# Sixty-four slots for four experts in place of three, wide and narrow experts in turn, and a narrow block's transposes inside the next block's products

## The chip, the cores and the metric

The kernel runs on one core of a Trainium2 chip. The time is that of one execution on the device, in microseconds (us). A profile is one execution taken by the hardware profiler; its times are counted from the first instruction of the span. PE is the matrix engine (TensorE), PEld its weight load, DVE the vector engine, ACT the scalar engine, POOL GpSimd, and SP the engine that issues the loads.

## The reference

A two-layer network on 256 latent and 256 context tokens of 1024 numbers in fp32. Layer 0 (scans and a dense feed-forward part) and the attention of layer 1 are not touched by the change. What it touches is the last stage: each of the 256 latent tokens goes to two of eight experts, and every expert has its own weights.

```python
def swiglu(h, w_gate, w_up, w_down):
    return (jax.nn.silu(h @ w_gate) * (h @ w_up)) @ w_down

def moe(h, w_router, w_gate, w_up, w_down):
    logits = (h @ w_router).astype(jnp.float32)
    top_val, top_idx = lax.top_k(logits, TOP_K)          # TOP_K = 2
    top_w = jax.nn.softmax(top_val, axis=-1)
    combine = jnp.sum(jax.nn.one_hot(top_idx, N_EXPERTS, dtype=jnp.float32) * top_w[..., None], axis=-2)
    out = jnp.zeros_like(h)
    for e in range(N_EXPERTS):                           # 8 experts, 1024 x 3584 gate, up; 3584 x 1024 down
        out = out + combine[..., e:e + 1].astype(h.dtype) * swiglu(h, w_gate[e], w_up[e], w_down[e])
    return out
```

With the reference's own inputs (seed 0) its routing sends 60, 52, 39, 90, 48, 47, 107 and 69 tokens to experts 0 to 7.

## The kernel before, in words

**Slots.** An expert's tokens are gathered into slots. `sorted` ranks the experts by their number of tokens (expert 0 always first, the others by falling count), so that number n in the program is a place in that ranking and `ids` holds which expert it is. `SLOTS` gives each place 128 slots (`CAP`) or 64 (`HALF`), and `ORDER` says in which order the places are worked through. In this kernel places 0 to 4 have 128 slots and places 5 to 7 have 64. Where an expert has more tokens than slots, `more` is above zero and a second pass under `tc.If(more > 0)` at the end of `experts` does the rest.

**Wide and narrow.** `expert` (128 slots, called wide here) splits each 128x1024 fp32 piece of weights into two fp32r parts (`wsplit`, ACT L183 and DVE L184) and multiplies three times (`mm3`, L194 to L196). `expert_half` (64 slots, called narrow) multiplies the fp32 weights as they are (L1427 gate and up, L1445 down), the two halves of the output's partitions side by side; the trace shows each such product as two records. Both work in the same steps: seven blocks of gate and up, each of eight 128x1024 pieces; the gather of the next expert (`gather`, L1351 to L1367); 28 pieces of down; and then the spreading of the result over the tokens (L1510 and L1511, or L1458) and its sum (`moe`).

**A narrow block.** After a block's products, ACT takes the silu (L1430), DVE multiplies (L1432), PE transposes twice (L1435) and ACT stores the transposed block in `ef` (L1436), from which down reads it.

**Weights.** `raw2` loads two pieces (1024 KB, written 1 MB below) at a time, on SP's queue (L1388, and L176 as two loads of 512 KB). The places are used in a ring of ten such units: two in the `raw` buffers and eight in four `wide` tiles of two units each. A load waits on SP until the unit that was there is used up. An expert has 42 units (28 gate and up, 14 down); 42 x 1024 KB are 44.04 MB. SP issues strictly in order, and the order of the units does not depend on which experts are narrow.

The order of instructions on each engine is set by a scheduler that takes the program's order as priority, so pieces of one step can stand inside another.

Of the kernel before, what the change touches and what calls it, by code (L numbers as in the profile page):

```python
# [13 lines left out]
I32 = mybir.dt.int32  # L14
AF = mybir.ActivationFunctionType
# [4 lines left out]
P = 128  # L20
# [5 lines left out]
NE = 8  # L26
CAP = P
HALF = 64

ORDER = (0, 1, 7, 2, 6, 3, 4, 5)  # L30
SLOTS = (CAP,) * 5 + (HALF,) * 3
FE = 3584
LAM_INIT = 0.8 - 0.6 * math.exp(-0.3)

# [1128 lines left out]
class Layer1Experts(Layer1):  # L1163
# [72 lines left out]
    def experts(self):  # L1236
        nc = self.nc
        v = nc.vector
        self.nraw, self.wide, self.al_slot, self.rest_slot = -5, (2, 3, 0, 1), 4, 4
        self.place, self.eid = self.rank, [0] * NE  # L1240
        g = self.gather(0, 0)
        self.sorted()
        for i, n in enumerate(ORDER):
            if n:
                self.eid[n] = nc.values_load(self.ids[0:1, n:n + 1], engines=[mybir.EngineType.SP],
                                             min_val=0, max_val=NE - 1)
            nxt = ORDER[i + 1] if i + 1 < NE else None
            run = self.expert if SLOTS[n] == CAP else self.expert_half
            g = run(n, g, 0, nxt, not i, nxt is None)

        more = nc.values_load(self.more[0:1, 0:1], min_val=0, max_val=256)
        with self.tc.If(more > 0):
            self.nraw, self.wide, self.al_slot = 0, (3, 0, 1), 2
            for n in range(NE):
                self.expert(n, self.gather(n, SLOTS[n]), SLOTS[n], None, not n, False)
            for t in range(2):
                for j in range(2):
                    c = slice(512 * j, 512 * j + 512)
                    u = self.scr("s3")
                    v.tensor_tensor(u, self.moe[:, t, c], self.rest[:, 2, c], op=ALU.mult)  # L1260
                    self.put(t, c, u)

    def sorted(self):

        nc = self.nc
        v = nc.vector
        room = self.pc.tile([P, 384], F32, name="order", tag="dt_ex")
        at = [0]

        def new(shape):  # L1270
            n = math.prod(shape)
            at[0] += n
            r = room[:, at[0] - n:at[0]]
            return r.rearrange("p (a b) -> p a b", b=shape[1]) if len(shape) == 2 else r

        e8 = lambda ap: ap[:, None, :].to_broadcast([P, NE, NE])
        io = self.con[:, C_IO:C_IO + NE]
        pn = self.tr()
        for t in range(2):
            nc.tensor.matmul(pn[:, 0:NE], self.con[:, C_ONE:C_ONE + P], self.sel[:, t, :], start=t == 0, stop=t == 1)  # L1280
        cnt, key, pos = (new([NE]) for _ in range(3))
        v.tensor_copy(cnt, pn[:, 0:NE])
        v.tensor_copy(key, pn[:, 0:NE])
        v.tensor_scalar(key[:, 0:1], key[:, 0:1], 1024.0, None, op0=ALU.add)
        cmp = self.scr("s3", (P, 2, NE, NE))
        mine, other = key[:, :, None].to_broadcast([P, NE, NE]), e8(key)
        v.tensor_tensor(cmp[:, 0], other, mine, op=ALU.is_equal)
        v.tensor_tensor(cmp[:, 1], other, mine, op=ALU.is_gt)
        v.tensor_tensor(cmp[:, 0], cmp[:, 0], self.con[:, C_TIE:C_TIE + NE * NE].rearrange("p (a b) -> p a b", b=NE),
                        op=ALU.mult)  # L1290
        v.tensor_reduce(pos, cmp.rearrange("p i a b -> p a i b"), axis=AX.XY, op=ALU.add)
        v.tensor_scalar(pos, pos, 1.0, None, op0=ALU.add)

        hot = new([NE, NE])
        v.tensor_tensor(hot, e8(pos), io[:, :, None].to_broadcast([P, NE, NE]), op=ALU.is_equal)
        self.place, self.wts = (new([2, NE]) for _ in range(2))
        num = new([2, NE])
        u = self.scr("s3", (P, 2, NE, NE))
        for src, dst in ((self.rank, self.place), (self.cw, self.wts)):
            v.tensor_tensor(u, src[:, :, None, :].to_broadcast([P, 2, NE, NE]),  # L1300
                            hot[:, None].to_broadcast([P, 2, NE, NE]), op=ALU.mult)
            v.tensor_reduce(dst, u, axis=AX.X, op=ALU.add)
        v.tensor_tensor(u[:, 0], e8(io), hot, op=ALU.mult)
        v.tensor_tensor(u[:, 1], e8(cnt), hot, op=ALU.mult)
        v.tensor_reduce(num, u, axis=AX.X, op=ALU.add)
        v.tensor_scalar(num[:, 0], num[:, 0], -1.0, None, op0=ALU.add)
        self.ids = new([NE]).bitcast(I32)
        v.tensor_copy(self.ids, num[:, 0])
        for lo, hi, cap in ((0, 5, CAP), (5, NE, HALF)):
            v.tensor_scalar(num[:, 1, lo:hi], num[:, 1, lo:hi], -float(cap), None, op0=ALU.add)  # L1310
        top = new([1])
        v.tensor_reduce(top, num[:, 1], axis=AX.X, op=ALU.max)
        v.tensor_scalar(top, top, 0.0, None, op0=ALU.max)
        self.more = new([1]).bitcast(I32)
        v.tensor_copy(self.more, top)
# [89 lines left out]
    def expert_half(self, n, gathered, base, nxt, first, final):  # L1405

        nc = self.nc
        v = nc.vector
        mm = nc.tensor.matmul
        xg, pT, w_tok = gathered  # L1410
        sides = [slice(HALF * i, HALF * i + HALF) for i in range(2)]
        if final:
            self.rest = self.big(self.rest_slot, (P, 3, D), name="rest")
            self.row("odd", 5, 0, self.rest[:, 2])
        ap = self.big(5, (P, FE // P, HALF), name="ef")
        for b in range(FE // 512):
            if final and 2 <= b < 6:
                self.so_far(b - 2)
            ps = self.mm(b % 4)
            for u in range(0, KD, 2):  # L1420
                raw = self.raw2(self.weights("exp_gu", n, b, u // 2))
                for i in range(2):
                    k = u + i
                    for g in range(2):
                        for h, s in enumerate(sides):
                            c = 512 * g + 256 * h
                            mm(ps[s, 256 * g:256 * g + 256], xg[:, k, :], raw[i][:, c:c + 256],  # L1427
                               start=k + g == 0, stop=k == KD - 1, skip_group_check=True)
            sg = self.scr("s0", (P, 256))
            nc.scalar.activation(sg, ps[:, 0:256], AF.Silu)  # L1430
            t = self.scr("s3", (P, 256))
            v.tensor_tensor(t, sg, ps[:, 256:512], op=ALU.mult)  # L1432
            pt = self.tr()
            for f in range(2):
                nc.tensor.transpose(pt[:, P * f:P * f + P], t[:, P * f:P * f + P], self.ident)  # L1435
            nc.scalar.activation(ap[:, 4 * b:4 * b + 4, :].rearrange("p (h f) s -> p f h s", h=2),  # L1436
                                 pt[:, 0:256].rearrange("p (f h s) -> p f h s", f=2, h=2), AF.Copy)
        out = self.gather(nxt, base) if nxt is not None else None
        py = self.acc()
        nd = FE // P  # L1440
        for u in range(0, nd, 2):
            raw = self.raw2(self.weights("exp_d", n, u // 2))
            for f in (u, u + 1):
                for j, s in enumerate(sides):
                    mm(py[s], ap[:, f, :], raw[f - u][:, 512 * j:512 * j + 512], start=f == 0, stop=f == nd - 1,  # L1445
                       skip_group_check=True)
        y = self.scr("s2")
        if final:
            for j, s in enumerate(sides):
                v.scalar_tensor_tensor(y[s], py[s], w_tok[s], self.rest[s, 2, 512 * j:512 * j + 512],  # L1450
                                       op0=ALU.mult, op1=ALU.mult)
        else:
            nc.scalar.activation(y, py, AF.Copy, scale=w_tok)
        for t in range(2):
            for j, s in enumerate(sides):
                c = slice(512 * j, 512 * j + 512)
                pt = self.tr()
                mm(pt, pT[s, P * t:P * t + P], y[s], start=True, stop=True)  # L1458
                if final:
                    self.put(t, c, pt)  # L1460
                else:
                    v.tensor_tensor(self.moe[:, t, c], self.moe[:, t, c], pt, op=ALU.add)
        return out
# [73 lines left out]
```

## Time and profile before

| | |
|---|---|
| time, median of 3 runs | 2052.66 us (2048.9 to 2054.36) |
| the profiled execution's own time | 2045.38 us |
| its span | 2043.6 us |
| PE busy | 1973.8 us, 97% of the span |
| DVE, ACT busy | 1332.9 us, 997.5 us |
| moved by DMA | 502.69 MB, mean 246 GB/s |
| granted TensorE clock, mean | 0.991 of full speed |

The eight experts are the last 45% of the span. The profiled execution lies 1.8 us above its span and 7.3 us below the median of the runs. A busy share is an average over stages with different limits; the stages of the experts are read apart, by windows of time that begin with an expert's first product.

### The profile page before, as it was taken

What the parts mean: (1) busy time and instruction counts of PE and PEld (TensorE: products, weight loads), DVE (VectorE), ACT (ScalarE), POOL (GpSimd) and SP (SyncE); (2) the same over time, 40 slices, a digit from 0 to 9 for tenths busy, and PEclk for the clock granted to TensorE, in tenths of its full rate; (3) what the DMA queues carried; (4) which work ended last, traced back from release to release, by engine and by line L of the source; (5) the groups of instructions that cost most, each with busy time, mean ns of one, the idle gap of its engine ahead of it and who ended that gap; (6) DMA issues with size and microseconds to landing.
All of it is one profiled execution on the core that took longest, in us unless ns stands there. A gap on an engine that the chain in (4) does not pass through costs nothing.

```text
span 2043.6 us, 26783 instructions
## 1 busy us (share of the span) xinstructions
PE 1973.8 (97%) x9852; PEld 1496.0 (73%) x9852; DVE 1332.9 (65%) x2199; ACT 997.5 (49%) x1460; POOL 10.1 (0%) x12
## 2 busy tenths in 40 slices
PE   7999999999999999999999999998999999999997
PEld 4777778786888888877758787875488547888752
DVE  5468579755865565678566989960498109899700
ACT  5544346633332222255454887751487117888610
POOL 0000000000000000000000000000000000000010
PEclk9999999999999999999988999999999999999999
DMA  8333433433544555434405789989999999999897
GB/s 324 109 98 103 135 134 126 165 117 133 177 159 163 183 175 175 137 103 125 164 15 203 272 339 351 372 326 418 417 417 370 368 417 418 364 368 366 329 383 322
DMA packets 103867, 502.69 MB, mean 246 GB/s; under 512 B 13104, under 2 KB 13744, under 8 KB 69296
## 3 DMA queue, kind: packets, MB, share of 16 engines
q1 hardware_dynamic: 103728, 500.91, 65.5%
q8 instruction: 79, 1.29, 0.3%
q14 instruction: 60, 0.49, 0.1%
HBM read 495.62 MB, written 5.24 MB: 245 GB/s over the span
## 4 chain that ended last, share of the span: by engine, by line
PE 84%; DVE 7%; DMA 5%; ACT 3%; issue 1%; SPq 0%; ACTq 0%; DVEq 0%
PE mm L195 18%; PE mm L196 18%; PE mm L194 18%; PE mm L1427 7%; DMA wide<-exp_d 4%; PE acc L195 3%; PE acc L196 3%; PE acc L194 3%; DVE lo L184 2%; PE acc L315 1%; PE tr L1351 1%; PE acc L1445 1%; PE mm L1138 1%; PE tr L817 1%; PE acc L954 1%
## 5 line engine op out<-in xcount | busy, mean ns | idle before, releaser
L183 ACT ACTIVATE hi<-raw 128x1024 fp32r<-128x1024 f32 x240 | 254.0, 1060 | 411.1 <-PE mm L196 203.1
L184 DVE TENSOR_TENSOR lo<-wide,hi 128x1024 fp32r<-128x1024 f32 x336 | 407.5, 1223 | 42.3 <-ACT hi L183 15.7
L184 DVE TENSOR_TENSOR lo<-raw,hi 128x1024 fp32r<-128x1024 f32 x240 | 292.0, 1221 | 178.3 <-ACT hi L183 171.0
L183 ACT ACTIVATE hi<-wide 128x1024 fp32r<-128x1024 f32 x336 | 354.9, 1061 | 91.5 <-PE mm L196 59.5
L195 PE MATMUL mm<-lo,q 128*128 128x512 f32 x560 | 221.7, 396 | 2.3 <-DVE lo L184 2.3
L196 PE MATMUL mm<-hi,q 128*128 128x512 f32 x560 | 219.8, 393 | 0.0
L194 PE MATMUL mm<-hi,q 128*128 128x512 f32 x560 | 199.0, 392 | 0.0
L194 PE MATMUL mm<-hi,hh 128*128 128x512 f32 x416 | 168.8, 407 | 1.7 <-DVE b L856 1.3
L195 PE MATMUL mm<-lo,hh 128*128 128x512 f32 x416 | 164.9, 396 | 0.0
L196 PE MATMUL mm<-hi,hl 128*128 128x512 f32 x416 | 163.8, 396 | 0.0
L194 PE MATMUL mm<-h2h,hi 128*128 128x512 f32 (+1 forms) x376 | 142.2, 378 | 1.3 <-ACT hi L183 1.3
L195 PE MATMUL mm<-h2l,hi 128*128 128x512 f32 (+1 forms) x376 | 141.5, 377 | 0.0
L196 PE MATMUL mm<-h2h,lo 128*128 128x512 f32 (+1 forms) x376 | 141.1, 376 | 0.0
L1427 PE MATMUL mm<-wide,q 128*64 128x256 f32 x1072 | 127.6, 382 | 0.0
L195 PEld LDWEIGHTS mm<-lo,q 128*128 128x128 f32 x560 | 105.6, 189 | 29.7 <-DVE lo L184 7.0
L194 PEld LDWEIGHTS mm<-hi,q 128*128 128x128 f32 x560 | 105.3, 188 | 24.6 <-issue 1.6
L196 PEld LDWEIGHTS mm<-hi,q 128*128 128x128 f32 x560 | 105.7, 189 | 21.4 <-issue 0.8
L195 PE MATMUL acc<-lo,eh 128*128 128x512 f32 x280 | 110.2, 394 | 0.8 <-DVE lo L184 0.7
L1432 DVE TENSOR_TENSOR s<-s,mm 128x256 f32<-128x256 f32 x21 | 8.8, 421 | 154.7 <-ACT s L1430 154.7
L196 PE MATMUL acc<-hi,el 128*128 128x512 f32 x280 | 109.6, 391 | 0.0
L1427 PEld LDWEIGHTS mm<-wide,q 128*64 128x64 f32 x1072 | 77.1, 137 | 41.9 <-issue 6.0
L194 PE MATMUL acc<-hi,eh 128*128 128x512 f32 x280 | 101.9, 389 | 0.0
(392 smaller groups left out, 3301.5 us busy)
## 6 DMA issues: line engine op xcount, KB each, us to landing
wide<-exp_gu SPq DMA_DIRECT2D x177, 1024.0 KB, 8.9
wide<-exp_d SPq DMA_DIRECT2D x91, 1024.0 KB, 9.4
raw<-exp_gu SPq DMA_DIRECT2D x92, 512.0 KB, 10.0
raw<-odd_wmod SPq DMA_DIRECT2D x48, 512.0 KB, 4.4
raw<-w_in SPq DMA_DIRECT2D x44, 512.0 KB, 3.7
raw<-ffn_gu SPq DMA_DIRECT2D x44, 512.0 KB, 4.4
raw<-exp_d SPq DMA_DIRECT2D x42, 512.0 KB, 13.9
raw<-even_wmod SPq DMA_DIRECT2D x36, 512.0 KB, 3.7
```

The lines of the kernel that those rows point to most:

```text
L183: nc.scalar.activation(hi, raw, AF.Copy)
L184: nc.vector.tensor_tensor(lo, raw, hi.bitcast(F32), op=ALU.subtract)
L194: mm(ps, lh, rh, start=first, stop=False, skip_group_check=skip)
L195: mm(ps, lh, rl, start=False, stop=False, skip_group_check=skip)
L196: mm(ps, ll, rh, start=False, stop=last, skip_group_check=skip)
L315: nc.tensor.matmul(ps[r:r + 32, :], self.cond[:, k, :], raw[:, 512 * kk:512 * kk + 512], start=k < 4, stop=k >= 4)
L817: nc.tensor.matmul(pe, m, r.rearrange("p h l -> p (h l)"), start=d + i == 0, stop=d + i == 2)
L954: nc.tensor.matmul(py[:, w], l, r, start=i == 0, stop=i == len(prod) - 1)
L1138: nc.tensor.matmul(ps, self.qT1[r, h, qs], self.kT1[r, h, :], start=True, stop=True)
L1351: nc.tensor.matmul(pt[:, w * kk:w * kk + w], self.x[:, 2 + t, P * (k + kk):P * (k + kk) + P], pn[:, t, 0:w], start=t == 0, stop=t == 1)
L1427: mm(ps[s, 256 * g:256 * g + 256], xg[:, k, :], raw[i][:, c:c + 256], start=k + g == 0, stop=k == KD - 1, skip_group_check=True)
L1445: mm(py[s], ap[:, f, :], raw[f - u][:, 512 * j:512 * j + 512], start=f == 0, stop=f == nd - 1, skip_group_check=True)
```

## The change

Place 4 gets 64 slots instead of 128; the order of the places becomes 0, 7, 1, 6, 2, 5, 3, 4, so that a narrow expert follows each wide one. In a narrow expert, transposes and the store of block b are called between the second and the third pair of pieces of block b + 1, and those of the last block after the next expert's gather. The second pass takes only the experts that have tokens left (`extra`), and is cleared first.

```diff
-ORDER = (0, 1, 7, 2, 6, 3, 4, 5)
-SLOTS = (CAP,) * 5 + (HALF,) * 3
+ORDER = (0, 7, 1, 6, 2, 5, 3, 4)
+SLOTS = (CAP,) * 4 + (HALF,) * 4
...
         with self.tc.If(more > 0):
             self.nraw, self.wide, self.al_slot = 0, (3, 0, 1), 2
+            for t in range(2):
+                v.memset(self.moe[:, t, :], 0.0)
             for n in range(NE):
-                self.expert(n, self.gather(n, SLOTS[n]), SLOTS[n], None, not n, False)
+                extra = nc.values_load(self.extra[0:1, n:n + 1], min_val=-P, max_val=256)
+                with self.tc.If(extra > 0):
+                    self.expert(n, self.gather(n, SLOTS[n]), SLOTS[n], None, False, False)
...
-        for lo, hi, cap in ((0, 5, CAP), (5, NE, HALF)):
+        for lo, hi, cap in ((0, 4, CAP), (4, NE, HALF)):
             v.tensor_scalar(num[:, 1, lo:hi], num[:, 1, lo:hi], -float(cap), None, op0=ALU.add)
+        self.extra = new([NE]).bitcast(I32)
+        v.tensor_copy(self.extra, num[:, 1])
...
         ap = self.big(5, (P, FE // P, HALF), name="ef")
+        def turn(b, t):
+            pt = self.tr()
+            for f in range(2):
+                nc.tensor.transpose(pt[:, P * f:P * f + P], t[:, P * f:P * f + P], self.ident)
+            nc.scalar.activation(ap[:, 4 * b:4 * b + 4, :].rearrange("p (h f) s -> p f h s", h=2),
+                                 pt[:, 0:256].rearrange("p (f h s) -> p f h s", f=2, h=2), AF.Copy)
+
+        t = None
         for b in range(FE // 512):
...
                 raw = self.raw2(self.weights("exp_gu", n, b, u // 2))
+                if t is not None and u == 4:
+                    turn(b - 1, t)
...
             v.tensor_tensor(t, sg, ps[:, 256:512], op=ALU.mult)
-            pt = self.tr()
-            for f in range(2):
-                nc.tensor.transpose(pt[:, P * f:P * f + P], t[:, P * f:P * f + P], self.ident)
-            nc.scalar.activation(ap[:, 4 * b:4 * b + 4, :].rearrange("p (h f) s -> p f h s", h=2),
-                                 pt[:, 0:256].rearrange("p (f h s) -> p f h s", f=2, h=2), AF.Copy)
         out = self.gather(nxt, base) if nxt is not None else None
+        turn(FE // 512 - 1, t)
         py = self.acc()
```

**Where the instructions stand.** PE in the middle of the first narrow expert, before: a block is 32 products (`mm_...`), and behind its last one stand the two transposes of the same block's activations (`s_...`, L1435).

```order
L1435 MATMUL tr<-con,s_11475 128x128 x2
L1427 MATMUL mm_11481<-wide,q_10905 64x256 x32
L1435 MATMUL tr<-con,s_11522 128x128 x2
L1427 MATMUL mm_11528<-wide,q_10905 64x256 x8
L1427 MATMUL mm_11528<-raw,q_10905 64x256 x16
L1427 MATMUL mm_11528<-wide,q_10905 64x256 x8
L1435 MATMUL tr<-con,s_11574 128x128 x2
```

The same place with the change (products L1443, transposes L1425):

```order
L1443 MATMUL mm_10229<-wide,q_9806 64x256 x8
L1425 MATMUL tr<-con,s_10227 128x128 x2
L1443 MATMUL mm_10229<-wide,q_9806 64x256 x16
L1443 MATMUL mm_10279<-wide,q_9806 64x256 x16
L1425 MATMUL tr<-con,s_10277 128x128 x2
L1443 MATMUL mm_10279<-wide,q_9806 64x256 x16
L1443 MATMUL mm_10326<-wide,q_9806 64x256 x8
L1443 MATMUL mm_10326<-raw,q_9806 64x256 x8
L1425 MATMUL tr<-con,s_10324 128x128 x2
```

A block's transposes now stand 16 products into the next block; in later blocks the scheduler puts some of them 4 products in, or at the block's start.

PE at the end of gate and up of that expert, before: transposes, the next expert's gather (L1351 to L1367), then down (`acc`).

```order
L1427 MATMUL mm_11580<-wide,q_10905 64x256 x32
L1435 MATMUL tr<-con,s_11621 128x128 x2
L1351 MATMUL tr<-s_11630,x 128x128 x16
L1365 MATMUL tr<-con,m_11627 128x128 x2
L1367 MATMUL tr<-order,m_11627 128x1 x2
L1445 MATMUL acc<-wide,ef 64x512 x12
```

With the change (gather L1357 to L1373, down L1457):

```order
L1443 MATMUL mm_10474<-raw,q_9806 64x256 x4
L1425 MATMUL tr<-con,s_10472 128x128 x2
L1357 MATMUL tr<-s_10527,x 128x128 x2
L1443 MATMUL mm_10474<-raw,q_9806 64x256 x4
L1357 MATMUL tr<-s_10527,x 128x128 x10
L1443 MATMUL mm_10474<-wide,q_9806 64x256 x8
L1357 MATMUL tr<-s_10527,x 128x128 x4
L1371 MATMUL tr<-con,m_10524 128x128 x2
L1373 MATMUL tr<-order,m_10524 128x1 x2
L1443 MATMUL mm_10474<-wide,q_9806 64x256 x16
L1425 MATMUL tr<-con,s_10522 128x128 x2
L1457 MATMUL acc<-wide,ef 64x512 x20
```

The gather has moved into the last block, and the last block's transposes stand right behind its products with nothing between them and down.

## Rows read from the trace of the kernel before

**Rows 1.** The page: chain that ended last by engine; DMA and GB/s by slice.

```profile
PE 84%; DVE 7%; DMA 5%; ACT 3%; issue 1%; SPq 0%; ACTq 0%; DVEq 0%
...
DMA  8333433433544555434405789989999999999897
GB/s 324 109 98 103 135 134 126 165 117 133 177 159 163 183 175 175 137 103 125 164 15 203 272 339 351 372 326 418 417 417 370 368 417 418 364 368 366 329 383 322
```

**Rows 2.** Windows by expert: us, busy by engine, clock, DMA share, GB/s.

```profile
1239.90:1365.50 125.60, 125.26 (x580) 101.82 (x578) 112.15 (x107) 97.80 (x110) 0.00 (x0) 1.00 0.93 349
1365.50:1459.40 93.90, 86.73 (x622) 46.36 (x621) 8.36 (x18) 13.30 (x33) 0.00 (x0) 1.00 0.99 404
1459.40:1586.90 127.50, 126.65 (x577) 101.97 (x576) 112.24 (x105) 96.60 (x107) 0.00 (x0) 1.00 0.98 396
1586.90:1683.70 96.80, 88.63 (x623) 47.29 (x622) 8.95 (x18) 13.77 (x34) 0.00 (x0) 1.00 0.98 395
1683.70:1812.10 128.40, 127.68 (x577) 103.43 (x577) 114.59 (x108) 99.78 (x110) 0.00 (x0) 0.99 0.97 390
1812.10:1937.80 125.70, 124.98 (x579) 102.45 (x577) 111.33 (x104) 97.47 (x111) 0.00 (x0) 1.00 0.92 350
1937.80:2032.70 94.90, 84.70 (x591) 42.84 (x590) 7.21 (x15) 7.91 (x19) 9.90 (x8) 1.00 0.94 379
2032.70:2043.60 10.90, 3.95 (x8) 1.18 (x8) 4.22 (x6) 0.00 (x0) 0.00 (x0) 0.85 0.29 102
```

**Rows 3.** SP's own waits, of the wide expert from 1239.9 to 1365.5 us.

```profile
SPq L1388 <- DVE lo L184: 94.0, 18, 9.6
```

**Rows 4.** PE's waits (us in total, times, longest): first narrow expert, then the last.

```profile
PE tr L1435 <- DVE s L1432: 5.2, 6, 0.9
PE acc L1445 <- DMA wide<-exp_d: 1.1, 2, 0.6
...
PE acc L1445 <- DMA wide<-exp_d: 4.0, 7, 0.7
```

**Rows 5.** Windows inside experts, columns as in rows 2.

```profile
1365.00:1380.00 15.00, 14.94 (x108) 7.97 (x108) 4.56 (x8) 2.41 (x6) 0.00 (x0) 1.00 0.88 334
1380.00:1459.00 79.00, 71.89 (x520) 38.53 (x516) 4.30 (x10) 10.49 (x26) 0.00 (x0) 1.00 1.02 418
1462.00:1546.00 84.00, 83.63 (x375) 67.30 (x374) 78.21 (x75) 66.73 (x72) 0.00 (x0) 1.00 1.02 418
1546.00:1587.00 41.00, 40.66 (x199) 33.68 (x198) 31.63 (x29) 28.65 (x34) 0.00 (x0) 1.00 0.90 350
...
1686.00:1688.80 2.80, 2.80 (x7) 2.20 (x8) 2.60 (x3) 1.60 (x2) 0.00 (x0) 0.50 1.02 421
```

**Rows 6.** Timeline of PE in the first narrow expert: start, us, what, [idle before].

```profile
1410.15 0.44 PE L1435 MATMUL tr<-con,s 128*128 128x128 f32 x2 [0.94 <-DVE s L1432]
...
1418.95 7.13 PE L1427 MATMUL mm<-wide,q 128*64 128x256 f32 x64
1427.02 0.44 PE L1435 MATMUL tr<-con,s 128*128 128x128 f32 x2 [0.94 <-DVE s L1432]
1427.29 3.74 PE L1351 MATMUL tr<-s,x 128*128 128x128 f32 x32
```

**Rows 7.** Timeline of PE in down of the narrow experts.

```profile
1440.18 10.66 PE L1445 MATMUL acc<-wide,ef 128*64 128x512 f32 x48
...
2026.38 1.94 PE L1445 MATMUL acc<-wide,ef 128*64 128x512 f32 x8 [0.46 <-DMA wide<-exp_d]
2028.98 1.94 PE L1445 MATMUL acc<-wide,ef 128*64 128x512 f32 x8 [0.67 <-DMA wide<-exp_d]
2030.72 1.92 PE L1445 MATMUL acc<-raw,ef 128*64 128x512 f32 x8
```

## The prediction

> **What bounds the kernel now.** I read the chain of waits and the page's slices first. The chain is PE for 84%, but DMA, which idles in most of the kernel, is at 9 tenths almost throughout the experts, with two levels: about 417 GB/s and about 350 to 370 [rows 1]. So the experts have two limits that take turns, and PE's 97% busy says little; each expert has to be read in its own window.
>
> In a window per expert [rows 2], wide ones take 125.6 and 125.7 us behind another wide one, and 127.5 and 128.4 us behind a narrow one. PE is busy for all but 0.3 to 0.9 us of that: PE bounds a wide expert. DMA then moves 349 or 350 GB/s, and not for want of speed: SP waits 94.0 us of such an expert for DVE to finish with a unit, which is the ring being full [rows 3]. Narrow ones take 93.9, 96.8 and, for the last, 94.9 us, with PE busy 8 to 10 us less than that [rows 2].
>
> Is a narrow expert bounded by PE or by its loads? Both nearly. PE idles 5.2 us in it for the transposes, which wait for DVE's product, and 1.1 us (4.0 us in the last one) for loads of down [rows 4]. But within it DMA runs at 334 GB/s for the first 15 us and then at 418 GB/s for 79 us, to its end [rows 5]. 418 is the highest level that any stretch of the experts shows, and it holds for 84 us in the wide expert that follows as well. A unit of 1.049 MB takes 2.5 us at that rate, and products of down that wait for loads do start 2.5 us apart (2026.38 and 2028.98, with 1.94 us of work each), while unhindered PE needs 10.66 / 6 = 1.78 us a unit [rows 7]. So a narrow expert eats a full ring and then lives on 418 GB/s: it now ends as its last loads land.
>
> **The change, part by part.**
>
> *Place 4 becomes narrow, and the order alternates.* Both together turn wide, wide, narrow, wide, narrow, wide, wide, narrow into four pairs. The first wide expert stays as it is and ends at 1239.9. From there to the last product of down it now takes 792.8 us: 125.6 + 93.9 + 127.5 + 96.8 + 128.4 + 125.7 + 94.9 [rows 2]. After the change there are three narrow ones that have a successor, three wide ones behind a narrow one, and the last narrow one. I take 93.9 for the narrow one behind the first wide one (there too the ring is full), 96.8 and the mean 95.35 for the next two, 3 x 127.95 (mean of 127.5 and 128.4) for the wide ones and 94.9 for the last: 764.8 us. That is 28.0 us less. The tail of 10.9 us behind the last product stays [rows 2].
>
> The condition is that the ring is full again when each narrow expert begins. The wide expert from 1459.4, which starts with it empty, shows that: it is filled at 418 GB/s until about 1546, and then falls to 350 GB/s, the pace of use, for the last 41 us [rows 5]. One wide expert is enough, with a third of it to spare.
>
> *The transposes move.* Per narrow expert nothing is added: the same 14 transposes and seven stores of ACT stand later. PE's stall at a block's end is 0.94 us, and the block itself 7.1 us [rows 6]; 16 products of 32 are half of that, so a wait of 0.94 is covered there, and mostly so where only four stand ahead. The last block's transposes have nothing behind the products to cover them: of 5.2 us, 0.94 stay and 4.3 go. ACT is busy 13.3 us of 93.9 [rows 2], so the store's new place there holds up nobody; only down reads it, and it reads the early blocks first. SP's loads keep their order, POOL's few instructions too. The gather (3.74 us of transposes on PE [rows 6]) moves into the last block; it is the same work on PE, and its cover for that block's stall is what is lost or won there, under 1 us.
>
> What are 4.3 us less of PE worth? What is late next is the loads. From 15 us after its start a narrow expert's DMA is already at 418 GB/s; products that come earlier only wait for loads earlier. Only the first 15 us can gain, where DMA ran at 334: (418 - 334) x 15 = 1.26 MB, or 3.0 us at 418. So the bounds are 0 and 3.0 us each as long as the loads set the end (4.3 if they do not). In those 15 us PE is busy 14.94 [rows 5], with the spreading of the wide result and a block that has no stall yet, and the change takes nothing out of that; so I take 0.5 us, 2.0 us for four.
>
> *Clock.* The second narrow expert ends in waits for loads, and in the wide one behind it the granted clock is 0.50 (1.2 GHz) for 2.8 us [rows 5], which costs 1.4 us; behind the first narrow one it does not fall [rows 2]. My mean has half of that in it. With more waits it may happen each time: 0 to 2 us more in all. I leave it in the range.
>
> *The second pass and `extra`.* The pass is skipped as long as no place overflows. One small DVE copy is added to the ranking, during the first wide expert; at worst SP reads the ranking one short instruction later, once. Nothing.
>
> **Sum:** -28.0 - 2.0 = -30.0 us. On the profiled execution: span 2013.6, own time 2015.4. The median of the runs lies 7.3 us above that execution; I put the same difference on the median: 2052.66 - 30.0 = 2022.7 us.
>
> **Rivals.**
>
> 1. *The loads are not a wall for the transposes*, and all of 4.3 us per narrow expert is gained: -28.0 - 17.2, 2007.5 us. For it: in the first narrow expert only two waits for loads, 1.1 us, are left [rows 4], so the wall is just touched. Against: 418 GB/s without a break for 79 us. 10%.
>
> 2. *The boundaries cost more.* There are seven between wide and narrow instead of five. If each wide expert behind a starved narrow one, and each start of a narrow one with its 15 us at 334 GB/s, costs 2 us more than the rows show, half the gain is gone: 2037 us. Against: three boundaries of the one kind and two of the other are in the sum as measured. 6%.
>
> 3. *No change, because loads are no faster for a narrow expert.* If 350 GB/s were what DMA can give and not the wide expert's pace, a narrow one would take 44.04 / 0.350 = 126 us in the long run, as much as the wide one it replaces, and only the ring's content, borrowed, made the three look shorter: about 2051 us. The 418 GB/s of whole stretches [rows 5] speak against it. The Trainium skill (DMA: Bandwidth & Descriptors, Specifications) states a limit of about 358 GB/s from HBM per core, which is this rival: by it an expert takes 123 us, wide or narrow, and the change brings nothing. This trace disagrees with that figure, 418 to 358, and the trace decides. 2%.
>
> 4. *Slower: the clock falls in the narrow experts.* Their place is down: more waits leave PE idle a quarter of the time, and at half clock a unit takes 3.56 us in place of 1.78, which is more than the 2.5 us of a load [rows 7]: 1.06 us lost per unit. With all 14 units of down at half clock that is 14.8 us, and 1.4 at the next start: four times 16 us, +65 - 30, 2088 us. It decides from 7 units a narrow expert on (30 / 4 / 1.06). Against: the last narrow expert has seven such waits in its 94.9 us and a clock of 1.00 [rows 2, 4]. The Trainium skill (TensorE: Matmul & The Clock Gate, The HAM clock gate) says that the throttled state is the default and activity releases it; the fall to 0.50 above agrees in kind. 3%.
>
> 5. *The change does more than it says:* place 4 overflows and the second pass runs. One wide expert, with nothing loaded ahead: 126 us at least, so 2052.66 - 30 + 126 = 2149 us. It decides at 65 tokens. By the reference's routing the fourth of places 1 to 7 has 52. 2%.
>
> **How the numbers follow.** My forecast has 77% (some 2012 to 2034), the rivals 10, 6, 2, 3 and 2. About 0.3% (6 us) is what a measurement of this kernel can tell from no change. Faster by more: forecast and rivals 1 and 2, 93%. Within: rival 3, 2%. Slower: rivals 4 and 5, 5%. The range, 2008 to 2034, takes in the bounds of the transposes (0 to 3.0 us each), the clock, some 4 us of difference between medians, and most of the way to rival 1; rivals 3 to 5, and part of 1 and 2, are outside.
>
> **What would show it.** In the new profile: four narrow experts of 93 to 97 us each and three wide ones of 127 to 129; PE's waits for DVE before the transposes down from 5.2 us to 1 or 2 in each narrow expert, and its waits for loads of down up by about as much, from 1 to 4 to 5 to 8; 418 GB/s from 15 us after a narrow start; about 350 at the end of each wide one. I am wrong if narrow experts take under 91 us or over 100, if waits for loads have not grown, or if a wide one behind a narrow one never comes down from 418 GB/s, which would mean that the ring is not refilled.

## The result, and the profile after

The changed kernel takes 2026.38 us (median of five runs, 2025.02 to 2030.33). Five runs of the kernel before, beside it, have a median of 2050.75 us (2043.43 to 2054.36). The ratio is 0.989, with a 95% interval of 0.987 to 0.991. That is 24.4 us faster between the medians; 30.0 was forecast, and the time lies in the range.

The profiled execution has a span of 2023.2 us. Its experts, window by window, answer to [rows 2] (us, busy by engine, clock, DMA share, GB/s). The first wide expert is left out, narrow and wide take turns, and the last row is the tail:

```profile
1244.30:1339.30 95.00, 87.72 (x622) 45.90 (x621) 8.43 (x18) 13.26 (x33) 0.00 (x0) 1.00 0.99 402
1339.30:1467.30 128.00, 126.93 (x578) 102.20 (x577) 112.50 (x106) 96.88 (x107) 0.00 (x0) 1.00 0.97 390
1467.30:1562.20 94.90, 86.96 (x622) 46.30 (x621) 8.53 (x18) 13.27 (x33) 0.00 (x0) 1.00 1.00 405
1562.20:1691.20 129.00, 128.13 (x577) 102.91 (x576) 112.35 (x105) 96.50 (x107) 0.00 (x0) 0.99 0.97 389
1691.20:1787.30 96.10, 88.53 (x623) 46.67 (x622) 8.94 (x18) 13.65 (x34) 0.00 (x0) 1.00 0.98 397
1787.30:1916.50 129.20, 128.12 (x577) 102.95 (x576) 111.68 (x103) 96.60 (x107) 0.00 (x0) 0.99 0.97 387
1916.50:2011.80 95.30, 84.46 (x591) 42.56 (x590) 7.18 (x14) 7.90 (x19) 9.93 (x8) 1.00 0.93 378
2011.80:2023.20 11.40, 3.95 (x8) 1.18 (x8) 4.25 (x6) 0.00 (x0) 0.00 (x0) 0.75 0.29 99
```

From the end of the first wide expert to the last product of down it is now 2011.8 - 1244.3 = 767.5 us, where it was 792.8: 25.3 us less. A wide expert of 125.7 us has gone and a narrow one of 95 has come. The first narrow expert begins 4.4 us later than the second wide expert, which stood in its place in the profile before (1244.3 against 1239.9); that comes from ahead of the experts, where the two programs do the same. In the profiles of this study the first product of the first wide expert starts anywhere from 1114.6 to 1122.9 us (before: 1114.9, changed: 1119.3, changed again: 1122.9), so the experts are compared from there on.

The loads inside experts answer to [rows 5]: the first 15 us of a narrow expert, the rest of it, the last 42 us of a wide one, a later narrow one after its first 15 us, and the starts of the second and third wide expert behind a narrow one.

```profile
1244.00:1259.00 15.00, 15.00 (x108) 7.99 (x107) 4.43 (x8) 2.03 (x5) 0.00 (x0) 1.00 0.88 340
1259.00:1337.00 78.00, 71.51 (x515) 37.62 (x514) 4.30 (x10) 9.47 (x25) 0.00 (x0) 1.00 1.01 414
...
1425.00:1467.00 42.00, 41.64 (x205) 34.58 (x203) 32.85 (x31) 29.91 (x35) 0.00 (x0) 1.00 0.89 334
...
1482.00:1560.00 78.00, 71.78 (x526) 38.67 (x522) 4.30 (x10) 9.08 (x24) 0.00 (x0) 1.00 1.02 414
...
1564.50:1567.20 2.70, 2.70 (x8) 2.12 (x8) 2.52 (x3) 0.11 (x1) 0.00 (x0) 0.53 1.00 416
...
1789.30:1792.30 3.00, 3.00 (x8) 2.27 (x8) 2.80 (x3) 0.66 (x2) 0.00 (x0) 0.50 1.02 410
```

So the ring is full again at the end of a wide expert (334 GB/s, the pace of use), and a narrow one lives on 414 GB/s after a slow start, as forecast. What was not forecast stands in PE's waits, which answer to [rows 4]: first, second, third and last narrow expert, the two longest groups of each (us in total, times, longest).

```profile
PE acc L1457 <- DMA wide<-exp_d: 3.5, 7, 0.6
PE tr L1425 <- DVE s L1448: 2.9, 3, 1.0
...
PE tr L1425 <- DVE s L1448: 5.7, 6, 1.0
PE acc L1457 <- DMA wide<-exp_d: 1.4, 1, 1.4
...
PE tr L1425 <- DVE s L1448: 5.7, 6, 1.0
PE acc L1457 <- DMA wide<-exp_d: 1.0, 2, 0.6
...
PE tr L1425 <- DVE s L1448: 5.6, 6, 0.9
PE acc L1457 <- DMA wide<-exp_d: 5.1, 8, 1.1
```

Before, it was 5.2 us of waiting for DVE in each of the first two narrow experts and 6.1 in the last. In three of four narrow experts next to nothing of that has gone. The timeline of PE in the last one shows why: the transposes (L1425) stand at the block's end or a few products behind it, not in the middle of the next block.

```profile
1938.97 0.44 PE L1425 MATMUL tr<-con,s 128*128 128x128 f32 x2 [0.94 <-DVE s L1448]
1939.34 5.40 PE L1443 MATMUL mm<-wide,q 128*64 128x256 f32 x48
1944.57 2.76 PE L1443 MATMUL mm<-raw,q 128*64 128x256 f32 x24
1947.40 0.44 PE L1425 MATMUL tr<-con,s 128*128 128x128 f32 x2
1947.77 1.08 PE L1443 MATMUL mm<-raw,q 128*64 128x256 f32 x8
1948.68 5.35 PE L1443 MATMUL mm<-wide,q 128*64 128x256 f32 x48
1954.97 0.44 PE L1425 MATMUL tr<-con,s 128*128 128x128 f32 x2 [0.94 <-DVE s L1448]
```

At 1947.40 eight records, four products, went ahead, and there is no wait; at 1938.97 and 1954.97 none did, and PE waits 0.94 us as before.

This left two theories for the gain. **L**: the loads set the end of a narrow expert; the whole gain is the swap of a wide expert for a narrow one, and the transposes are worth nothing as long as that holds. The rival, **T**: the moved transposes bring a part of it, or (**S**) would bring it if the scheduler had really moved them.

### The profile page after: what moved, and what is told of

It is laid out like the page before. It is cut to its first block, busy times and chain, and to the rows that moved or that the text cites. A ratio compares the mean times of both kernels' runs of the same rounds, so it can differ in the third digit from the quotient of the medians.

```text
span 2023.2 us, 26554 instructions
## 1 busy us (share of the span) xinstructions
PE 1943.0 (96%) x9894; PEld 1440.6 (71%) x9894; DVE 1225.9 (61%) x2105; ACT 906.3 (45%) x1373; POOL 10.1 (1%) x12
## 4 chain that ended last, share of the span: by engine, by line
PE 82%; DMA 7%; DVE 7%; ACT 3%; issue 1%; SPq 0%; ACTq 0%; DVEq 0%
PE mm L196 17%; PE mm L195 17%; PE mm L194 17%; PE mm L1443 9%; DMA wide<-exp_d 4%; PE acc L195 2%; PE acc L196 2%; PE acc L194 2%; DVE lo L184 2%; PE tr L1357 1%; PE acc L315 1%; PE acc L1457 1%; PE tr L1470 1%; PE mm L1138 1%; PE tr L817 1%
## 5 line engine op out<-in xcount | busy, mean ns | idle before, releaser
L184 DVE TENSOR_TENSOR lo<-wide,hi 128x1024 fp32r<-128x1024 f32 x268 | 324.7, 1223 | 34.8 <-ACT hi L183 14.1
L183 ACT ACTIVATE hi<-wide 128x1024 fp32r<-128x1024 f32 x268 | 282.5, 1061 | 75.2 <-PE mm L196 52.6
L195 PE MATMUL mm<-lo,q 128*128 128x512 f32 x448 | 177.8, 397 | 2.0 <-DVE lo L184 1.7
L196 PE MATMUL mm<-hi,q 128*128 128x512 f32 x448 | 176.0, 393 | 0.0
L1443 PE MATMUL mm<-wide,q 128*64 128x256 f32 x1424 | 168.7, 382 | 0.0
L194 PE MATMUL mm<-hi,q 128*128 128x512 f32 x448 | 159.1, 395 | 0.0
L1443 PEld LDWEIGHTS mm<-wide,q 128*64 128x64 f32 x1424 | 100.3, 137 | 55.1 <-issue 8.1
L194 PEld LDWEIGHTS mm<-hi,q 128*128 128x128 f32 x448 | 84.5, 189 | 23.9 <-issue 4.5
L194 PEld LDWEIGHTS mm<-hi,hh 128*128 128x128 f32 x416 | 78.4, 189 | 27.8 <-issue 9.7
L196 PEld LDWEIGHTS mm<-hi,q 128*128 128x128 f32 x448 | 84.8, 189 | 16.9
L1457 PE MATMUL acc<-wide,ef 128*64 128x512 f32 x360 | 82.4, 598 | 11.0 <-DMA wide<-exp_d 11.0
L196 PEld LDWEIGHTS mm<-hi,hl 128*128 128x128 f32 x416 | 78.5, 189 | 17.1 <-issue 0.8
```

The source lines that it names most:

```text
L183: nc.scalar.activation(hi, raw, AF.Copy)
L184: nc.vector.tensor_tensor(lo, raw, hi.bitcast(F32), op=ALU.subtract)
L194: mm(ps, lh, rh, start=first, stop=False, skip_group_check=skip)
L195: mm(ps, lh, rl, start=False, stop=False, skip_group_check=skip)
L196: mm(ps, ll, rh, start=False, stop=last, skip_group_check=skip)
```

## The experiments

All ratios are to the kernel before, run on the same chip, with 95% intervals.

### The swap alone

```diff
             v.tensor_tensor(t, sg, ps[:, 256:512], op=ALU.mult)
+            turn(b, t)
...
-                if t is not None and u == 4:
-                    turn(b - 1, t)
...
-        turn(FE // 512 - 1, t)
```

> The changed kernel with each block's transposes called in their old place; four narrow experts and the new order stay. Theory L (the loads set the end of a narrow expert, so the whole gain is the swap): 2026 us, within 5 us of the changed kernel, narrow experts 94 to 97 us each as there. Rival T (the moved transposes carry a part of the gain): slower than the changed kernel by at least 4 x 2 = 8 us, 2034 us or more, narrow experts 97 us or more.

Measured: 2025.2 us, ratio 0.9901 (0.9887 to 0.9915); before 2046.06. The narrow experts:

```profile
1241.80:1336.70 94.90, 87.43 (x623) 46.13 (x622) 8.36 (x18) 13.32 (x33) 0.00 (x0) 1.00 0.99 401
1464.70:1559.60 94.90, 86.56 (x622) 46.59 (x621) 8.53 (x18) 13.30 (x33) 0.00 (x0) 1.00 0.99 401
1688.60:1784.70 96.10, 87.81 (x624) 46.89 (x623) 8.96 (x18) 13.68 (x34) 0.00 (x0) 1.00 0.98 397
1913.90:2009.30 95.40, 84.88 (x591) 42.82 (x590) 7.18 (x14) 7.91 (x19) 9.90 (x8) 1.00 0.92 374
```

381.3 us for the four, the same as in the changed kernel (95.0 + 94.9 + 96.1 + 95.3 = 381.3). The swap and the new order are all of the gain that the experts show. T falls, as far as the scheduler had moved the transposes at all.

### The transposes alone

```diff
-ORDER = (0, 7, 1, 6, 2, 5, 3, 4)
-SLOTS = (CAP,) * 4 + (HALF,) * 4
+ORDER = (0, 1, 7, 2, 6, 3, 4, 5)
+SLOTS = (CAP,) * 5 + (HALF,) * 3
...
-        for lo, hi, cap in ((0, 4, CAP), (4, NE, HALF)):
+        for lo, hi, cap in ((0, 5, CAP), (5, NE, HALF)):
```

(a diff to the changed kernel)

> Three narrow experts and the order of the kernel before; only the transposes are called inside the next block. Theory L: 2051 us, no change within 5 us. Rival T: up to 3 x 4.3 = 13 us faster, 2038 us, with PE's waits for DVE before the transposes down to 1 us per narrow expert.

Measured: 2048.24 us, ratio 1.0008 (0.9999 to 1.0016): no change. The three narrow experts take 94.6, 97.0 and 95.6 us, against 93.9, 96.8 and 94.9 before, and PE's waits for DVE are still 4.8, 4.7 and 5.6 us. This says the same as the first run, but it does not part L from S, because here too the transposes hardly moved.

### The transposes really moved

```diff
             for f in range(2):
-                nc.tensor.transpose(pt[:, P * f:P * f + P], t[:, P * f:P * f + P], self.ident)
+                tr = nc.tensor.transpose(pt[:, P * f:P * f + P], t[:, P * f:P * f + P], self.ident)
+                if not f:
+                    self.tc.keep_in_program_order(tr)
```

> The changed kernel, with each pair of transposes pinned on PE behind the 16 products that stand before it in the program (in the changed kernel the scheduler had put most of them back to the block's end). PE's waits for DVE fall from 5.7 us to about 1 us per narrow expert in either theory. Theory L: PE's waits for loads grow by as much, narrow experts stay at 93 to 96 us, 2020 to 2027 us. Rival S (the transposes brought nothing only because they were not moved): narrow experts 90 to 92 us, 2009 to 2014 us.

Measured: 2020.33 us, ratio 0.9881 (0.9862 to 0.9899). PE's waits in the second narrow expert, where the wait for DVE stood at 5.7 us:

```profile
PE acc L1459 <- DMA wide<-exp_d: 4.2, 6, 1.4
PE tr L1472 <- ACT s L1467: 0.8, 1, 0.8
PE mm L1445 <- DMA wide<-exp_gu: 0.5, 1, 0.5
PE acc L1459 <- DMA raw<-exp_d: 0.3, 1, 0.3
```

No wait for DVE before the transposes is left in this one, nor in the first and third; the wait for loads is 5.0 us (4.2 + 0.5 + 0.3) instead of 1.4. And the expert is as long as it was. First and second narrow expert:

```profile
1240.50:1335.50 95.00, 88.52 (x622) 46.11 (x621) 8.53 (x18) 13.30 (x33) 0.00 (x0) 1.00 0.99 401
1463.60:1558.30 94.70, 88.82 (x622) 45.84 (x621) 8.59 (x18) 13.34 (x33) 0.00 (x0) 1.00 1.00 404
```

The third takes 96.6 and the last 93.8 us (96.1 and 95.3 in the changed kernel): 380.1 for the four, 1.2 us less. L holds; the wait has only changed its name. S falls. The median lies 4.9 us below that of the run with the swap alone, on the same chip, but the intervals overlap, and from the first narrow expert's start to the last product of down the two profiles differ by only 1.3 us (766.3 against 767.6).

### Two narrow experts in a row

```diff
-ORDER = (0, 7, 1, 6, 2, 5, 3, 4)
+ORDER = (0, 1, 7, 2, 6, 3, 5, 4)
```

> The changed kernel in the order 0, 1, 7, 2, 6, 3, 5, 4: the same four wide and four narrow experts, but two wide ones in a row at the start and two narrow ones in a row at the end. Theory L with the ring as its reserve: the last narrow expert begins with an empty ring and takes 44.04 MB / 0.418 = 105 us instead of 95; one wide expert less starts behind a narrow one (125.6 instead of 128.7): +10 - 3, 2033 us. Rival O (the order is worth nothing, only the number of narrow experts counts): 2023 us, with both narrow ones at 95.

Measured: 2030.72 us, ratio 0.9923 (0.9908 to 0.9939). The last two experts, both narrow:

```profile
1818.50:1914.70 96.20, 88.62 (x623) 46.97 (x622) 7.18 (x14) 10.27 (x28) 0.00 (x0) 1.00 0.98 396
1914.70:2018.90 104.20, 86.26 (x589) 40.66 (x588) 5.77 (x13) 6.84 (x17) 9.91 (x8) 1.00 0.98 401
```

96.2 us with a full ring, 104.2 with an empty one; 105 was expected. A narrow expert is 8 us shorter than its loads only because the wide one ahead has filled the ring for it. So the order is a part of the gain: the same four narrow experts gain less when two stand together. The intervals do not settle that alone (0.9908 here, up to 0.9915 with the swap alone); the profile does: from the end of the first wide expert to the last product of down it is 774.1 us here and 767.5 in the changed kernel.

### Half the loads

```diff
-    def raw2(self, ap):
+    def raw2(self, ap, half=False):
...
+            if half:
+                return [self.wraw(ap[:, 0:1024])] * 2
...
+        if half:
+            self.nc.sync.dma_start(t[:, 0], ap[:, 0:1024])
+            return [t[:, 0]] * 2
```

(`expert_half` passes `True`)

> The changed kernel, but each unit of a narrow expert loads only its first 512 KB and multiplies them twice (the second half of the narrow experts' weights is left out); products, waits and order stay. Theory L (the loads set the end of a narrow expert): PE's waits for loads (3.5, 1.4, 1.0 and 5.1 us in the four narrow experts of the changed kernel) go to zero and the experts shorten by about that; the granted clock no longer falls at the start of a wide one, so all three wide ones behind a narrow one take 128 us and none 129; about 13 us less, 2013 us. Rival P (narrow experts are bounded by PE, the loads just fit): no change, 2026 us.

> The same with half the narrow loads, and the transposes pinned inside the next block. Theory L: now that no load is waited for, the 4 to 5 us of waits for DVE that the pinning takes away come off each narrow expert: 89 to 90 us each, some 15 us less than with half the loads alone, 1998 us. Rival P: the same saving would have shown with full loads, where pinning left the narrow experts at 95 us; nothing more here, 2013 us.

Measured: 1980.64 us, ratio 0.9673 (0.9648 to 0.9698), and with the pinning 1978.47 us, 0.9662 (0.9638 to 0.9687). Both differ from what I expected, and in the same way: in both, the first two narrow experts take 85.3 us each, and the third and the last 85.9 and 82.6 us behind the last product of the wide one (two of their products stand ahead of that). The first, of the run without pinning:

```profile
1241.40:1326.70 85.30, 85.30 (x620) 46.36 (x619) 11.93 (x21) 14.50 (x33) 0.00 (x0) 1.00 0.77 261
```

PE is busy all through it, with no wait at all. The transposes, which had stood at the block's end in most blocks, now stand inside the next block without pinning (that the scheduler left them at the end because it took the loads to be late is my reading, and no run shows it); so the pinning had nothing left to do, and the pair could not price the transposes. The wide experts behind take 128.1, 128.5 and 128.5 us at a clock of 1.00, the last two with some 0.6 us of the next narrow one's products in them.

A third run with half the loads, therefore, holds the transposes at their own block's end:

```diff
+            turn(b, t)
...
+                            if b and k + g + h == 0:
+                                self.tc.keep_in_program_order(pr)
```

(`pr` is the block's first product; the transposes are pinned too)

> Half the narrow loads as before (the second half of the narrow experts' weights left out), but with the transposes pinned at the end of their own block. With half the loads the scheduler had moved the transposes by itself, and narrow experts took 85.3 us with no wait for DVE at all. Theory L (transposes cost their stall as soon as no load covers it): five to seven stalls of 0.94 us come back, narrow experts take 90 to 92 us, some 20 us more in all than with half the loads alone, 2000 us. Rival N (the place of the transposes is worth nothing even then): 85.3 us, 1980 us.

Measured: 1998.93 us, ratio 0.9747 (0.9710 to 0.9783). The first narrow expert and its only wait:

```profile
1243.20:1333.20 90.00, 85.31 (x621) 46.56 (x620) 11.90 (x21) 14.60 (x33) 0.00 (x0) 1.00 0.71 246
...
PE tr L1431 <- DVE s L1454: 4.7, 5, 0.9
```

90.0 us: five stalls, 4.7 us, one for one. So the edit is sound: it is worth 4.7 us an expert where no load is waited for, against a forecast of 4.3, and next to nothing where the loads set the end. The first two narrow experts give the four cases side by side: with all loads 94.9 and 94.9 us with the transposes called in their old place, 95.0 and 94.7 with them moved; with half the loads 90.0 and 90.0, and 85.3 and 85.3. So PE alone would need 85.3 us for a narrow expert.

### A deeper ring in the narrow experts

If loads are the wall, what is left is their slow start, 340 GB/s in the first 15 us, when the ring is full and SP is stopped. One buffer, slot 4, holds the second split of the activations in wide experts (`al`) and is idle in narrow ones; it has room for two units. In the first run they were a narrow expert's units 10 and 11:

```diff
+    def spare(self, ap, u):
+
+        if u == 4:
+            self.spare_raw = self.big(self.al_slot, (P, 4, 1024), name="wide")
+        t = self.spare_raw[:, u - 4:u - 2]
+        self.nc.sync.dma_start(t.rearrange("p u c -> p (u c)"), ap)
+        return [t[:, i] for i in range(2)]
...
-                raw = self.raw2(self.weights("exp_gu", n, b, u // 2))
+                w = self.weights("exp_gu", n, b, u // 2)
+                raw = self.spare(w, u) if b == 2 and u >= 4 and not final else self.raw2(w)
```

> The changed kernel with two more places in the ring during the three narrow experts that have a successor: their units 10 and 11 are loaded into the buffer that holds the second split of the activations in wide experts and lies idle in narrow ones, so that two loads can be issued at once when a narrow expert begins. Theory L: DMA no longer drops to 312 to 353 GB/s in the first 15 us, which is worth up to 3 us per narrow expert, but PE has only its 3.5, 1.4 and 1.0 us of waits for loads to lose: 3 to 6 us less in all, 2020 to 2023 us. Rival O (the ring's depth is not what holds the loads up): no change, 2026 us.

> The same two places more, and the transposes pinned. Theory L: each of the two edits makes room for the other: the loads end up to 3 us earlier per narrow expert and PE can follow; narrow experts 92 to 93 us, 8 to 12 us less than the changed kernel, 2014 to 2018 us. Rival O: as with the pinning alone, about 3 us less than the changed kernel, narrow experts at 95 us.

Measured: 2019.49 us, ratio 0.9870 (0.9850 to 0.9891), and with the pinning 2018.94 us, 0.9874 (0.9853 to 0.9895). From the changed kernel's 0.989 neither is clear. The first 15 us of the second and the third narrow expert, without pinning:

```profile
1461.00:1476.00 15.00, 14.07 (x89) 7.11 (x89) 4.65 (x8) 3.10 (x7) 0.00 (x0) 1.00 0.79 317
...
1686.00:1701.00 15.00, 14.06 (x95) 7.29 (x95) 4.65 (x8) 2.74 (x7) 0.00 (x0) 1.00 1.01 413
```

Only the third has lost its slow start, and it alone has become clearly shorter: 93.3 us (94.5 and 95.4 the others). SP issues in order; a wide tile holds two units and is free only when both are used, so it depends on the position in the ring whether SP stops at a narrow expert's unit 9 or 10. In the first two it was already stopped at unit 9, in front of the extra places: the two loads into them were issued at 1467.2 us in the second narrow expert, 5.3 us after its start, and at 1686.5 in the third, just ahead of its start. The next pair puts them where SP stops:

```diff
+        place = self.nraw % 10
+        first_spare = 9 if place > 2 and place % 2 else 10
...
+                i = 4 * b + u // 2 - first_spare
+                raw = self.spare(w, i) if i in (0, 1) and not final else self.raw2(w)
```

(`spare` as above, by `i`)

> The two places more in the ring, now used for the units at which SP is really stopped when a narrow expert begins (unit 9 or 10, by the position in the ring); in the run with units 10 and 11 that was so only for the third narrow expert, which took 93.3 us with 413 GB/s in its first 15 us, where the other two stayed at 94.5 and 95.4 us with 324 and 317 GB/s. Theory L: all three narrow experts have about 410 GB/s from the start; they are 1 to 3 us shorter each than in the changed kernel, 4 to 8 us less in all. Rival O (the third one was quicker by chance): the first two stay at 94.5 and 95.4 us.

> The same with the transposes pinned inside the next block. Theory L: PE can follow the earlier loads, narrow experts take 91.5 to 93 us; less is gained than that where the wide expert behind starts at a granted clock of 0.50 (2 to 3 us in the last such run): 5 to 10 us less than the changed kernel. Rival O: as with the pinning alone.

> The changed kernel once more, for a comparison on the same chip: ratio 0.989 to the kernel before in every theory, narrow experts 94.9 to 96.1 us.

Measured on one chip: the changed kernel again 2025.75 us, ratio 0.9880 (0.9853 to 0.9906); units in step 2017.26 us, 0.9842 (0.9816 to 0.9868); with the pinning 2015.82 us, 0.9826 (0.9799 to 0.9853). The medians lie 8.5 and 9.9 us below the changed kernel's; the interval of the pinned one ends where that of the changed kernel begins, that of the other overlaps it. The first 15 us of the three narrow experts, pinned, and then the first two whole:

```profile
1244.00:1259.00 15.00, 15.00 (x108) 8.08 (x106) 4.55 (x8) 2.03 (x5) 0.00 (x0) 1.00 1.01 406
1464.00:1479.00 15.00, 15.00 (x105) 8.12 (x104) 4.65 (x8) 2.36 (x6) 0.00 (x0) 1.00 0.98 398
1686.00:1701.00 15.00, 15.00 (x109) 8.23 (x111) 4.12 (x8) 2.34 (x6) 0.00 (x0) 1.00 1.02 416
1244.40:1336.20 91.80, 88.20 (x622) 46.37 (x621) 8.46 (x18) 13.08 (x33) 0.00 (x0) 1.00 1.01 415
1464.00:1556.30 92.30, 88.81 (x623) 46.87 (x622) 9.04 (x18) 13.62 (x34) 0.00 (x0) 1.00 1.01 414
```

398 to 416 GB/s from the start, and 91.8, 92.3 and 91.8 us, where the changed kernel, run again, has 95.0, 95.4 and 96.0. Without the pinning it is 92.5, 93.9 and 93.3 us, at 404, 396 and 406 GB/s. So the loads' slow start was worth 1.5 to 2.7 us a narrow expert by itself, about its price of 3 us, and with it out of the way the transposes are worth 0.7 to 1.6 us more. The last narrow expert, which got no extra places, is longer: 96.8 and 96.2 us against 95.0. From the first narrow expert's start to the last product of down the three profiles have 764.4 us (changed, again), 759.8 and 757.0; so 4.6 and 7.5 us are what the experts show, and the rest of the 8.5 and 9.9 us between the medians lies elsewhere. These are the quickest versions of the study that load all the weights.

## Why the prediction was right, and where it was off

**The limit** held. A narrow expert ends as its last loads land: taking PE's waits away leaves it as long (94.7 to 96.6 us), halving the loads takes it to 90.0 with the transposes at their block's end and to 85.3 with them moved, an empty ring to 104.2, and quicker first loads to 92.

**The swap**, -28.0 us, was the right term. Its parts: the four narrow experts were put at 380.95 us together before the transposes and took 381.3. The three wide ones were put at 3 x 127.95 = 383.85 and took 128.0 + 129.0 + 129.2 = 386.2. The 2.35 us more lie at the starts, at the granted clock of 0.50 and 0.53 shown above; I had left 0 to 2 us for that in the range. In the second profile of the changed kernel the clock did not fall there, and the three take 128.0, 127.4 and 127.6, 383.0 in all.

**The ring's refilling**, the condition of it all, held: 334 GB/s at a wide expert's end, and the run with two narrow experts in a row shows what its failing costs.

**The transposes**, -2.0 us, are the step that failed, in two places. "Of 5.2 us, 0.94 stay and 4.3 go" was wrong: 2.9, 5.7, 5.7 and 5.6 us stayed. I read the place of the transposes from the first narrow expert, and took from the few rows where they stand at a block's start that it was an exception; in the later experts it is the rule. One of the signs that I named for being wrong came with it: in the second and third narrow expert the waits for loads had not grown (1.4 and 1.0 us; 2.1 us in the middle one before), as PE was no earlier. That the change does not do what it says was a rival that I should have listed for this edit. It cost little because the second half of the step was right: what these microseconds are worth, 0 to 3.0 us, as loads come late next. It was 0 in the changed kernel, where little had moved, 0.3 on average when pinned (1.2 us over four, one profile of each), and 0.7 to 1.6 where the loads' start was quickened as well.

**The sum.** -28.0 - 2.0 was forecast; -25.3 is what the profiles show from the end of the first wide expert on: 2.0 of the difference are the transposes, 2.35 the clock, and 0.35 the narrow experts. That the 2.35 us are the clock is worked out, not tested: the second and third wide expert behind a narrow one are each 1.6 us longer than in the second profile, where it did not fall, and 2.7 us at 0.53 and 3.0 us at 0.50 cost 1.3 and 1.5 us by estimate. The medians differ by 24.4. That the time came within 3.7 us of the 2022.7 forecast, with a gain 5.6 us short, is 1.9 us of luck: the median before was 2052.66 when I forecast and 2050.75 beside the change. Two readings in the prediction were a little off without bearing on the sum: PE is busy 7 to 10 us less than a narrow expert's window, not 8 to 10, and the two starts quoted as 2.5 us apart are 2.6 apart (the five starts that end with them are 2.5 apart on average).

**The rivals.** *The loads are not a wall* fell with the pinned run. *No change, because loads are no faster for a narrow expert* (350 GB/s) fell with 414 GB/s for 78 us. The limit of about 358 GB/s that the Trainium skill (DMA: Bandwidth & Descriptors, Specifications) lists is, by the same row, the 716 GB/s of a stack divided by two cores. This program runs on one core, and its 414 GB/s lie above that share: the measurement decides, and the prediction took a share for a wall. *The clock falls in the narrow experts* did not happen: each of them has 1.00 in its window, with up to eight waits for loads of down; only the start of a wide one suffers. *The second pass* did not run: the tail behind the last product of down is 11.4 us, against 10.9. *The boundaries cost more* is the nearest to the truth, through the clock, at a sixth of the price I gave it.

**What the forecast took as it stood.** A wide expert behind a narrow one takes 128 us even with half the loads and a full clock, instead of 125.5. The forecast used this from the rows without a reason, and the traces show most of it. PE spreads the narrow result over the tokens in fp32, inside the next expert's start. First two of its eight records (PE L1475) and PE's next instruction, with half the loads; then two of a wide result's eight and the next, in the kernel before:

```profile
1327.86 1.12 PE L1475 MATMUL tr<-s,m 64*128 64x512 f32 x2
1328.91 0.50 PE L195 MATMUL mm<-lo,q 128*128 128x512 f32 x1
...
1242.50 0.40 PE L1510 MATMUL tr<-s,m 128*128 128x512 f32 x1
1242.73 0.40 PE L1511 MATMUL tr<-s,m 128*128 128x512 f32 x1
1242.97 0.39 PE L195 MATMUL mm<-lo,q 128*128 128x512 f32 x1
```

Counted from each start to PE's next start, the eight records take 4.2 us for the narrow result and 1.9 us for the wide one. PE idles at most 0.3 us in either expert, so that is 2.3 of the 2.6 us (128.1 against 125.5).

## What to carry to other kernels

Where two kinds of stage take turns, one bounded by an engine and one by loads, what counts is the buffer between them: let the first fill it for the second, and look at where the issuing queue stops when the second begins. A stall in a stage that ends with its last load is worth nothing until the loads come earlier, however plainly the profile shows it; do both edits or neither. And look in the order of the instructions whether a move in the program has moved anything, at every instance and not at the first.

## What the runs showed of the hardware

The granted clock can fall at the start of a densely busy stage, after waits that are each short. In the changed kernel the second wide expert behind a narrow one has 0.53 (close to the level of 1.2 GHz) for 2.7 us near its start, behind one wait for loads of 1.4 us and two of 0.8 and 0.4 for the spreading; the third has 0.50 for 3.0 us, behind two waits for loads of 0.6 us at most and the same two for the spreading; the first one, behind seven waits for loads of 0.6 us at most and the same two, does not fall; and in another execution of the same program neither the second nor the third did. What decides it stays open. With half the loads, and so without those waits, it did not fall at the start of any. In the run with two more units and pinned transposes it fell at the second wide expert's start for longer (0.58 over 7 us), and that expert took 131.2 us.

DMA into one core held 414 to 418 GB/s for stretches of 78 to 92 us, in narrow experts and, for 84 us, in a wide one.

A record of 64x512 in fp32, of the narrow result's spreading, holds PE for 0.53 us; one of 128x512 in a wide result's, among the products of a wide expert, for 0.23 us.
